# Half of the context tokens' second expert rows: gathered for two tokens at once and added by TensorE in place of VectorE

## The chip, the cores and the metric

The kernel runs on one core of a Trainium2 chip, in one launch. The metric is the time of one execution on the device, in microseconds (us). The engines named here are TensorE (PE in the profile, its weight loads PEld), VectorE (DVE), ScalarE (ACT), GpSimd (POOL) and SyncE (SP); the last two also hold queues from which transfers (DMA) are started.

## The reference

The kernel is one inference step of a two-layer trunk over 128 context tokens and 512 latent tokens of width 1024. In each layer a token mixer (a gated linear attention, a short convolution and a windowed attention, merged by three branch products) is followed by a layer of experts, PEER. What the change touches is that layer, for the context tokens:

```python
def peer_ffn(h, w_pq, keys, u_tab, v_tab):
    ...                                   # 8 heads, top 16 of 128*128 experts each
    gate = jax.nn.softmax(top_s, axis=-1)
    def block(args):
        xb, ib, gb = args                 # 128 tokens, their 8*16 expert indices and gates
        act = jax.nn.gelu(jnp.einsum('td,thkd->thk', xb, u_tab[ib]), approximate=False)
        return jnp.einsum('thk,thkd->td', gb * act, v_tab[ib])
```

So each token has 128 ranks (8 heads times 16). For every rank a row of 1024 numbers of `u_tab` is multiplied with the token (the first half of an expert), and a row of `v_tab` is added to the output with the weight gate times gelu (the second half).

## The kernel before

The tokens stand on the 128 partitions. For the 128 context tokens of a layer, `peer_gather` fetches rows by an indirect transfer from GpSimd's queue: `fetch` starts one transfer of 128 rows, one for each token (512 KB), into a buffer named `grow`. `u_row` (line 920) reads it with one VectorE instruction that multiplies and sums into a column of `w`; `v_row` (lines 930 and 932) reads it with one VectorE instruction that adds it to the accumulator `gacc`. A layer has 128 fetches of each kind, 256 in all, in a fixed sequence: 16 of u, then 16 of u and 16 of v by turns of a head. The use of a row stands one step (`LAG = 1`) behind its fetch, and five `grow` buffers go round (`n=5`).

This gather of layer l is a background generator. While the latent tokens' mixer of the same layer (`mixer_lat`) is written out, each of its products calls `tick()`, and for each tick so many steps of the gather are written between: `RATE`, which is 0.9, 5.5 and 2.464 steps a tick in layer 0 in the three stages (gated attention; windowed attention; branches and output product), and 0.84, 6.0 and 2.08 in layer 1. A tick of the branch stage is 24 matmuls of 512 columns. After that a scheduler orders each engine's instructions. VectorE's gather instructions are kept in program order (`pin`). The order of every engine is fixed when the program is built, and each engine takes its queue strictly in order: what stands behind an instruction that waits, waits too.

Beside the gather, VectorE, ScalarE and GpSimd split each weight unit into two parts in `w_unit` (lines 172 to 176; GpSimd does 5/16 of the low part in these stages), and TensorE takes three matmuls for each product of the latent tokens (lines 196 to 198). PSUM has four pairs of banks (`pa`, `po`, `pb`, `pt`); `pt` holds transposes. Matmuls of 32 columns at four column places of the array, which the change uses, are in the kernel before too: `modulation` (line 267) does them with float32 operands of 128x32 and 128x256.

Of the kernel before, what the change touches and what calls it, by code (L numbers as in the profile page):

```python
# [9 lines left out]
F32 = mybir.dt.float32  # L10
F32R = mybir.dt.float32r
BF16 = mybir.dt.bfloat16
I32 = mybir.dt.int32
U32 = mybir.dt.uint32
U8 = mybir.dt.uint8
AF = mybir.ActivationFunctionType
# [27 lines left out]
def kernel(ctx: ExitStack, tc: tile.TileContext, A: dict, O: list):  # L44
    nc = tc.nc
# [28 lines left out]
    def pt(shape, name="pt"):  # L74
        return psum.tile(shape, F32, tag="pt", name=name, bufs=2)

    act = nc.scalar.activation
    V = nc.vector


    idf = const.tile([128, 128], F32, name="idf")
# [31 lines left out]
    def behind(i, j):  # L113

        tc.add_manual_dep(i.ins, j.ins.name, mybir.DependencyInfo(mybir.DependencyClass.NoSync,
                                                                  mybir.DependencyReason.DATA))
# [662 lines left out]
    def top16(v, ix, x):  # L779
        V.max(v[:, 0:8], x)  # L780
        V.max_index(ix[:, 0:8], v[:, 0:8], x)
        V.match_replace(x, v[:, 0:8], x, NEG)
        V.max(v[:, 8:16], x)
        V.max_index(ix[:, 8:16], v[:, 8:16], x)

    def routing_keys(s, l, hH, hL, vals, idxs, qp):

        for u in range(8):
# [8 lines left out]
            for t in range(s.nt):  # L797
# [7 lines left out]
                    top16(vals[t][:, hp, :], idxs[t][:, hp, :], sc[:, f, :])  # L805
                yield

    def routing_pairs(t, vals, idxs, rp, qp, out):

        vf = vals[t].rearrange("p (h q) k -> p h q k", q=2)
        xf = qp.tile([128, 8, 2, 16], F32, name="xf", bufs=1)
        V.tensor_copy(xf.rearrange("p h q k -> p (h q k)"), idxs[t].rearrange("p h k -> p (h k)"))
        top = qp.tile([128, 8, 16], F32, name="top", bufs=1)
        pos = qp.tile([128, 8, 16], U32, name="pos", bufs=1)
        for h in range(0, 8, 2):
            hs = slice(h, h + 2)
            cand = qp.tile([128, 2, 256], F32, tag="oh", name="cand", bufs=1)[:, :, :136]
            V.tensor_add(cand[:, :, :128].rearrange("p h (a b) -> p h a b", b=16),  # L820
                         vf[:, hs, 0, :8, None].to_broadcast([128, 2, 8, 16]),
                         vf[:, hs, 1, None, :].to_broadcast([128, 2, 8, 16]))
            V.tensor_add(cand[:, :, 128:], vf[:, hs, 0, 8:], vf[:, hs, 1, 0:1].to_broadcast([128, 2, 8]))
            for i in range(2):
                top16(top[:, h + i, :], pos[:, h + i, :], cand[:, i, :])
            yield
        pf = qp.tile([128, 8, 16], F32, name="pf", bufs=1)
        V.tensor_copy(pf, pos)
        ab = qp.tile([128, 2, 8, 16], U32, name="ab", bufs=1)
        V.tensor_scalar(ab[:, 0], pos, 4, None, op0=OP.logical_shift_right)  # L830
        V.tensor_scalar(ab[:, 1], pos, 15, None, op0=OP.bitwise_and)
        abf = qp.tile([128, 2, 8, 16], F32, name="abf", bufs=1)
        V.tensor_copy(abf, ab)

        V.tensor_scalar(pf, pf, -128.0, 0.0, op0=OP.add, op1=OP.max)
        V.tensor_add(abf[:, 0], abf[:, 0], pf)
        V.tensor_sub(abf[:, 1], abf[:, 1], pf)
        sel = rp.tile([128, 2, 8, 16], F32, name="sel%d" % t)
        yield
        for q in range(2):  # L840
            for h in range(0, 8, 2):
                hs = slice(h, h + 2)
                oh = qp.tile([128, 2, 16, 16], F32, tag="oh", name="oh", bufs=1)
                V.tensor_tensor(oh, abf[:, q, hs, :, None].to_broadcast([128, 2, 16, 16]),
                                iota16[:, None, None, :].to_broadcast([128, 2, 16, 16]), op=OP.is_equal)
                V.tensor_mul(oh, oh, xf[:, hs, q, None, :].to_broadcast([128, 2, 16, 16]))
                V.reduce_sum(sel[:, q, hs, :], oh, axis=mybir.AxisListType.X)
                if h % 4 == 2:
                    yield
        flat3 = lambda v: v.rearrange("p h k -> p (h k)")  # L850
        eidx = None
        if t == 0:
            eidx = rp.tile([128, 8, 16], I32, name="eidx")
            V.scalar_tensor_tensor(eidx, sel[:, 0], 128.0, sel[:, 1], op0=OP.mult, op1=OP.add)
            eidx = flat3(eidx)
        gate = rp.tile([128, 8, 16], F32, name="gate%d" % t)
        V.tensor_sub(gate, top, top[:, :, 0:1].to_broadcast([128, 8, 16]))
        act(gate, gate, AF.Exp)
        gs = qp.tile([128, 8], F32, name="gs", bufs=1)
        V.reduce_sum(gs, gate, axis=mybir.AxisListType.X)  # L860
        V.reciprocal(gs, gs)
        V.tensor_mul(gate, gate, gs[:, :, None].to_broadcast([128, 8, 16]))
        out[t] = (eidx, flat3(gate), flat3(sel[:, 0]), flat3(sel[:, 1]))
        yield
# [18 lines left out]
    gcfg = {}  # L883

    def peer_gather(s, l, t, eidx, gate, gp, out=None, after=None):
        h = gp.tile([128, D], F32, name="gh", bufs=1)
        def row():
            return gcfg["p"].tile([128, D], F32, tag=gcfg["tag"], name="grow", bufs=gcfg["n"])

        def mrow(j):  # L890
            t_ = row()
            m = modrow[l][s.idx, j * D:(j + 1) * D]
            nc.sync.dma_start(t_, bass.AP(tensor=m.tensor, offset=m.offset, ap=[[0, 128], [1, D]]))
            return t_

        sc, sh = mrow(4), mrow(3)
        x = s.x[t]
        if not s.ctx:
            x = row()
            nc.sync.dma_start(x, xdr[s.name][:, t, :])  # L900
        i = V.scalar_tensor_tensor(h, sc, 1.0, x, op0=OP.add, op1=OP.mult)
        if after:
            behind(i, after)
        V.tensor_add(h, h, sh)
        acc = gp.tile([128, D], F32, name="gacc", bufs=1)
        junk = gp.tile([128, D], BF16, name="gjunk", bufs=1)
        w = gp.tile([128, 128], F32, name="gw", bufs=1)

        def pin(i):
            if PIN[gcfg["m"]]:  # L910
                tc.keep_in_program_order(i)

        def fetch(tab, j):
            g = row()
            nc.gpsimd.indirect_dma_start(out=g, out_offset=None, in_=A[tab + str(l)],  # L915
                                         in_offset=bass.IndirectOffsetOnAxis(ap=eidx[:, j:j + 1], axis=0))
            return g

        def u_row(j, g):
            pin(V.scalar_tensor_tensor(junk, g, 1.0, h, op0=OP.mult, op1=OP.mult, accum_out=w[:, j:j + 1]))  # L920
            if j % 16 == 15:
                ws = w[:, j - 15:j + 1]
                act(ws, ws, AF.Gelu)

        def v_row(j, g):
            if j % 16 == 0:
                ws = w[:, j:j + 16]
                V.tensor_mul(ws, ws, gate[:, j:j + 16])
            if j == 0:
                pin(V.tensor_scalar(acc, g, w[:, j:j + 1], None, op0=OP.mult))  # L930
            else:
                pin(V.scalar_tensor_tensor(acc, g, w[:, j:j + 1], acc, op0=OP.mult, op1=OP.add))  # L932


        rows = []
        for hd in range(9):
            r = range(hd * 16, hd * 16 + 16)
            rows += [(u_row, "peer_u", j) for j in r if hd < 8] + [(v_row, "peer_v", j - 16) for j in r if hd]
        todo = []
        for i in range(len(rows) + LAG):  # L940
            if i < len(rows):
                todo.append(fetch(*rows[i][1:]))
            if i >= LAG:
                use, _, j = rows[i - LAG]
                use(j, todo.pop(0))
            yield
        if s.ctx:
            peer_add(s, t, [acc], mrow(5), acc)
            normalize(s, [t])
        else:  # L950
            out.append(acc)
# [199 lines left out]
    def run(gen):  # L1151
        for _ in gen:
            pass
# [101 lines left out]
    LAG = 1  # L1255
# [75 lines left out]

    for l in range(DEPTH):
        with pool("g_ctx") as gp:
            gcfg.update(p=gp, tag="grow", n=5, m=0)
            with w_pool(2, 2, PL[1]):
                if l:
                    lat.open_cv()
                    run(lat.finish(l))
                    e = bg_add(peer_gather(C, l, 0, ro_c[0], ro_c[1], gp, after=lat.end), RATE[l][0], PR[2])
                    mixer_lat(l, e, range(4))  # L1340
                else:
                    first = First(gp)
                    e = bg_add(first.work(), RATE[0][0], PR[2])
                    mixer_lat(l, e, range(CONV[0], 4), first)
            bg_drain(e)
# [4 lines left out]
        with pool("e_lat") as ep:  # L1350
            hH, hL = lat.h
            vals, idxs = route_bufs(Lt, ep)
# [156 lines left out]
```

## Time and profile before

| | |
|---|---|
| median of 3 runs | 5698.48 us (5694.15 to 5700.12) |
| the profiled execution | 5700.02 us, its span 5698.2 us |
| TensorE busy | 5144.1 us (90%) |
| VectorE busy | 4257.4 us (75%) |
| GpSimd busy | 2493.1 us (44%) |
| ScalarE busy | 2052.4 us (36%) |
| mean granted TensorE clock | 0.951 of full speed |

The span is what the profiler saw from the first to the last instruction; the execution's own time is 1.8 us longer. Busy shares are means over stages with different limits, so the argument goes by stretches of the span. The context gather of layer 0 runs from 574 us to about 1425 us, that of layer 1 from 3243 us to about 4198 us.

### The profile page before, as it was taken

The page shows a single profiled execution, that of the slowest core. Times are in us where ns is not written, and L with a number is a line of the kernel's source. Part 1 is how long each engine was busy: PE and PEld are TensorE (multiplying, and loading weights), DVE is VectorE, ACT ScalarE, POOL GpSimd, SP SyncE. Part 2 cuts the span into 40 slices and gives each one's busy share as a digit, 9 for nine tenths or more (in the row PEclk, how much of TensorE's full clock was granted, in tenths as well). Part 3 has the DMA queues.
Part 4 walks back from the last instruction along what each step waited for, and adds up shares of the span by engine and source line. Part 5 has one row for each costly group of instructions (what it writes and reads, how often), then busy time and mean ns, then how long its engine had stood idle before and what let it go on. Part 6 is the DMA issues. An engine that isn't in the chain of part 4 may idle for free. (4 is left out here: it accounts for less than half of the span.)

```text
span 5698.2 us, 78492 instructions
## 1 busy us (share of the span) xinstructions
PE 5144.1 (90%) x28598; PEld 4475.9 (79%) x28598; DVE 4257.4 (75%) x7555; ACT 2052.4 (36%) x3456; POOL 2493.1 (44%) x1907
## 2 busy tenths in 40 slices
PE   8998899888899998899999788999989788899997
PEld 6887778767788998888777677777778788799876
DVE  3328878878554868887777798888879998677667
ACT  2214434221232226653333344332223457333332
POOL 1112434676210007876555533456750466444332
PEclk9999999999899999999999899999989899999999
DMA  7762457887666667899999533678842776888895
GB/s 293 269 240 94 156 176 231 297 293 259 212 213 237 226 229 269 307 338 323 325 309 325 186 132 123 225 258 294 293 158 101 233 266 246 310 273 271 285 320 198
DMA packets 456708, 1395.09 MB, mean 245 GB/s; under 512 B 42880, under 2 KB 184832, under 8 KB 413312
## 3 DMA queue, kind: packets, MB, share of 16 engines
q1 hardware_dynamic: 303248, 833.73, 41.3%
q0 software_dynamic: 153072, 556.34, 28.7%
q8 instruction: 225, 3.69, 0.3%
q14 instruction: 163, 1.34, 0.1%
HBM read 1275.29 MB, written 114.62 MB: 244 GB/s over the span
## 5 line engine op out<-in xcount | busy, mean ns | idle before, releaser
L915 POOL DMA_INDIRECT grow<-in_peer_u_dram,eidx x512 | 689.1, 1346 | 675.8 <-DVE gjunk L920 235.8
L915 POOL DMA_INDIRECT grow<-in_peer_v_dram,eidx x512 | 669.3, 1307 | 630.2 <-DVE gacc L932 282.5
L932 DVE SCALAR_TENSOR_TENSOR gacc<-grow,gw,gacc 128x1024 f32<-128x1024 f32 x508 | 707.1, 1392 | 94.8 <-DMA grow<-in_peer_v_dram,eidx 89.8
L176 POOL TENSOR_TENSOR wl<-wraw,wh 128x640 fp32r<-128x640 f32 (+1 forms) x260 | 417.0, 1606 | 703.0 <-ACT wh L172 646.9
L920 DVE SCALAR_TENSOR_TENSOR gjunk<-grow,gh 128x1024 bf16<-128x1024 f32 x512 | 678.1, 1324 | 60.8 <-DMA grow<-in_peer_u_dram,eidx 56.6
L172 ACT ACTIVATE wh<-wraw 128x1024 fp32r<-128x1024 f32 (+1 forms) x388 | 515.2, 1342 | 522.8 <-PE pa L197 207.4
L174 DVE TENSOR_TENSOR wl<-wraw,wh 128x1408 fp32r<-128x1408 f32 (+2 forms) x388 | 555.5, 1434 | 177.2 <-ACT wh L172 177.0
L196 PE MATMUL acc<-wh,daH 128*128 128x512 f32 x1536 | 610.9, 398 | 60.3 <-ACT daH L110 43.8
L198 PE MATMUL acc<-wh,daL 128*128 128x512 f32 x1536 | 612.7, 399 | 14.6 <-DVE daL L111 14.3
L197 PE MATMUL acc<-wl,daH 128*128 128x512 f32 x1536 | 608.4, 396 | 0.5 <-DVE wl L174 0.5
L196 PE MATMUL pa<-hH,wh 128*128 128x512 f32 x1312 | 544.0, 415 | 48.0 <-DVE th L742 12.3
L198 PE MATMUL pa<-hH,wl 128*128 128x512 f32 x1312 | 536.5, 410 | 7.2 <-DVE wl L174 7.2
L197 PE MATMUL pa<-hL,wh 128*128 128x512 f32 x1312 | 536.8, 409 | 0.5 <-DVE hL L111 0.4
L196 PE MATMUL po<-hH,uH 128*128 128x384 f32 x1376 | 490.5, 356 | 26.6 <-ACT uH L1012 10.6
L198 PE MATMUL po<-hH,uL 128*128 128x384 f32 x1376 | 476.6, 347 | 18.4 <-DVE uL L1014 18.1
L197 PE MATMUL po<-hL,uH 128*128 128x384 f32 x1376 | 474.5, 345 | 0.0
L1012 ACT ACTIVATE uH<-uraw 128x1024 fp32r<-128x1024 f32 x256 | 270.8, 1058 | 563.3 <-PE po L197 192.7
L196 PEld LDWEIGHTS acc<-wh,daH 128*128 128x128 f32 x1536 | 294.2, 192 | 130.6 <-ACT daH L110 55.3
L1014 DVE TENSOR_TENSOR uL<-uraw,uH 128x1024 fp32r<-128x1024 f32 (+1 forms) x256 | 285.4, 1115 | 120.0 <-ACT uH L1012 120.0
L985 POOL TENSOR_SCALAR ob<-iota,tt,tt 128x128 f32<-128x128 f32 x192 | 299.3, 1564 | 172.6 <-ACT tt L966 91.8
L198 PEld LDWEIGHTS acc<-wh,daL 128*128 128x128 f32 x1536 | 294.2, 192 | 94.3 <-DVE daL L111 33.4
L196 PEld LDWEIGHTS pa<-hH,wh 128*128 128x128 f32 x1312 | 255.3, 195 | 115.6 <-DVE th L742 14.3
(365 smaller groups left out, 11788.5 us busy)
## 6 DMA issues: line engine op xcount, KB each, us to landing
wraw<-in_w_in_dram SPq DMA_DIRECT2D x168, 1024.0 KB, 5.7
uraw<-in_u_T_dram SPq DMA_DIRECT2D x256, 512.0 KB, 4.7
wraw<-in_v_n_dram SPq DMA_DIRECT2D x256, 512.0 KB, 6.1
wraw<-in_w_mod_dram SPq DMA_DIRECT2D x48, 1024.0 KB, 6.0
wraw<-in_w_branch_dram SPq DMA_DIRECT2D x48, 1024.0 KB, 5.6
gdr<-stage SPq DMA_DIRECT2D x24, 2048.0 KB, 10.4
G<-gdr SPq DMA_DIRECT2D x64, 768.0 KB, 8.0
sdr<-ust SPq DMA_DIRECT2D x172, 192.0 KB, 4.4
```

The lines of the kernel that those rows point to most:

```text
L172: act(H, raw, AF.Copy)
L174: V.tensor_sub(L[:, :m], raw[:, :m], H[:, :m].bitcast(F32))
L176: nc.gpsimd.tensor_sub(L[:, m:], raw[:, m:], H[:, m:].bitcast(F32))
L196: nc.tensor.matmul(out, aH, bH, start=start, stop=False)
L197: nc.tensor.matmul(out, aH, bL, start=False, stop=False)
L198: nc.tensor.matmul(out, aL, bH, start=False, stop=stop)
L915: nc.gpsimd.indirect_dma_start(out=g, out_offset=None, in_=A[tab + str(l)], in_offset=bass.IndirectOffsetOnAxis(ap=eidx[:, j:j + 1], axis=0))
L920: pin(V.scalar_tensor_tensor(junk, g, 1.0, h, op0=OP.mult, op1=OP.mult, accum_out=w[:, j:j + 1]))
L932: pin(V.scalar_tensor_tensor(acc, g, w[:, j:j + 1], acc, op0=OP.mult, op1=OP.add))
L985: (nc.gpsimd if w == "P" else V).tensor_scalar(ob[:, k, :], iota128, TT[1][:, j:j + 1], TT[2][:, j:j + 1], op0=OP.is_equal, op1=OP.mult)
L1012: act(uH, raw, AF.Copy)
L1014: V.tensor_sub(uL[:, :m, :], raw[:, :m, :], uH[:, :m, :].bitcast(F32))
```

## The change

For the context tokens, the second halves of ranks 0 to 63 are fetched in another shape. One fetch brings the 64 rows of token 2f on partitions 0 to 63 and those of token 2f+1 on partitions 64 to 127 (64 such fetches of 512 KB instead of 64 fetches of one rank for 128 tokens; the indices come from `pairs_below`, a TensorE transpose and two VectorE copies). `pair_row` adds them up with TensorE: four float32 matmuls of 128x32 by 128x256, one for each quarter of the width, each at its own column place, whose stationary operand `gdiag` holds the weights of the two tokens in two columns. Sixteen such fetches fill 32 tokens in one PSUM tile `pg` of the `pt` pair; then ScalarE copies it out and four transfers of SyncE's queue put it into `gacc`. The sequence of a layer's 256 fetches is now: 64 of u; 64 times one of u and one pair; 64 of v for ranks 64 to 127, which VectorE adds as before. The use stands two steps behind its fetch instead of one, and there are four `grow` buffers instead of five. The latent tokens' gather keeps its sequence.

```diff
+    def pairs_below(dst, src, copy):
+        p = pt([128, 128], name="pp")
+        nc.tensor.transpose(p, src, idf)
+        for i in range(2):
+            hs = slice(64 * i, 64 * i + 64)
+            copy(dst[hs, :], p[hs, i::2])
...
+            if len(vals) == 1:
+                ef = qp.tile([128, 2, 64], F32, name="pf", bufs=1)
+                V.tensor_copy(ef, eidx[:, None, :64].to_broadcast([128, 2, 64]))
+                e2 = rp.tile([128, 64], I32, name="eidx2")
+                pairs_below(e2, ef.rearrange("p i k -> p (i k)"), V.tensor_copy)
+                eidx = eidx, e2
...
+        def pair_row(f, g):
+            b, i = divmod(f, 16)
+            if f == 0:
+                w2 = gp.tile([128, 2, 64], F32, name="gw2", bufs=1)
+                V.tensor_mul(w2, w[:, None, :64].to_broadcast([128, 2, 64]),
+                             gate[:, None, :64].to_broadcast([128, 2, 64]))
+                wT = gp.tile([128, 64], F32, name="gwT", bufs=1)
+                pairs_below(wT, w2.rearrange("p i k -> p (i k)"), V.tensor_copy)
+                diag = gp.tile([128, 16 * 32], F32, name="gdiag", bufs=1)
+                nc.gpsimd.memset(diag, 0.0)
+                pr.update(w=wT, diag=diag)
+            diag = pr["diag"]
+            if i == 0:
+                for h in range(2):
+                    hs = slice(64 * h, 64 * h + 64)
+                    act(diag[hs, h::34], pr["w"][hs, 16 * b:16 * b + 16], AF.Copy)
+                pr["p"] = pt([128, 256], name="pg")
+            for c in range(4):
+                nc.tensor.matmul(pr["p"][32 * c:32 * c + 32, :], diag[:, 32 * i:32 * i + 32],
+                                 g[:, 256 * c:256 * c + 256], start=i == 0, stop=i == 15,
+                                 tile_position=(0, 32 * c), skip_group_check=True)
+            if i == 15:
+                st = gp.tile([128, 256], F32, name="gst", bufs=1)
+                act(st, pr["p"], AF.Copy)
+                for c in range(4):
+                    nc.sync.dma_start(acc[32 * b:32 * b + 32, 256 * c:256 * c + 256], st[32 * c:32 * c + 32, :])
...
-        for hd in range(9):
-            r = range(hd * 16, hd * 16 + 16)
-            rows += [(u_row, "peer_u", j) for j in r if hd < 8] + [(v_row, "peer_v", j - 16) for j in r if hd]
+        lag = LAG
+        if s.ctx:
+            lag = 2
+            eidx, e2 = eidx
+            rows = [(u_row, "peer_u", eidx, j) for j in range(64)]
+            for j in range(64):
+                rows += [(u_row, "peer_u", eidx, j + 64), (pair_row, "peer_v", e2, j)]
+            rows += [(v_row, "peer_v", eidx, j) for j in range(64, 128)]
...
-            gcfg.update(p=gp, tag="grow", n=5, m=0)
+            gcfg.update(p=gp, tag="grow", n=4, m=0)
```


The scheduler's order shows what this does on two engines.

GpSimd's queue, in the branch stage of layer 0, before. `DMASW0` to `DMASW7` are eight counters that successive fetches use in turn; the counter in a fetch's wait is that of the fetch that filled its buffer the last time, `DVE` or `PE` is the engine that read it then. `wl` is GpSimd's part of a weight unit.

```order
L915 DMA grow<-in_peer_u_dram,eidx 128x1024 [waits DMASW5_49,DVE_49]
L915 DMA grow<-in_peer_u_dram,eidx 128x1024 [waits DMASW6_49,DVE_49]
L915 DMA grow<-in_peer_u_dram,eidx 128x1024 [waits DMASW7_49,DVE_49]
L915 DMA grow<-in_peer_u_dram,eidx 128x1024 [waits DMASW0_49,DVE_49]
L176 TENSOR_TENSOR wl<-wraw,wh 128x640 [waits DMAHW2_49,PE_49,Activation_49]
L915 DMA grow<-in_peer_u_dram,eidx 128x1024 [waits DMASW1_49,DVE_49]
L915 DMA grow<-in_peer_u_dram,eidx 128x1024 [waits DMASW2_49,DVE_49]
```

And in the changed program (`eidx_4315` is `eidx2`, the indices of the pairs):

```order
L930 DMA grow<-in_peer_u_dram,eidx 128x1024 [waits DMASW7_49,DVE_49]
L176 TENSOR_TENSOR wl<-wraw,wh 128x640 [waits DMAHW7_49,Activation_49]
L930 DMA grow<-in_peer_v_dram,eidx_4315 128x1024 [waits DMASW4_49,PE_49]
L930 DMA grow<-in_peer_u_dram,eidx 128x1024 [waits DMASW1_49,DVE_49]
L930 DMA grow<-in_peer_v_dram,eidx_4315 128x1024 [waits DMASW6_49,PE_49]
L930 DMA grow<-in_peer_u_dram,eidx 128x1024 [waits DMASW3_49,DVE_49]
L930 DMA grow<-in_peer_v_dram,eidx_4315 128x1024 [waits DMASW0_49,PE_49]
L176 TENSOR_TENSOR wl<-wraw,wh 128x640 [waits DMAHW3_49,Activation_49]
L930 DMA grow<-in_peer_u_dram,eidx 128x1024 [waits DMASW5_49,DVE_49]
L930 DMA grow<-in_peer_v_dram,eidx_4315 128x1024 [waits DMASW2_49,PE_49]
```

Before, each fetch waits for the fetch five places back, whose row VectorE read. Now a fetch of u waits for the fetch two places back, which is the fetch of u before it: the waits of the u fetches go up by two (7, 1, 3, 5), as their own counters do. The u rows pass through one buffer here, and the pairs go round in the other three, each waiting for TensorE.

TensorE's queue, in the windowed attention of layer 0, in the changed program (`pa` is a product of the convolution; before, the same rows stand without the fifth):

```order
L198 MATMUL pa<-hH,wl 128x512
L196 MATMUL pa<-hH,wh 128x512
L197 MATMUL pa<-hL,wh 128x512
L198 MATMUL pa<-hH,wl 128x512
L970 MATMUL pg<-grow,gdiag 32x256 x12
L196 MATMUL pa<-hH,wh 128x512
L197 MATMUL pa<-hL,wh 128x512
```

Four matmuls are one pair row, so three pair rows stand here in a row. In the branch stage one pair row stands behind every 24 matmuls of 512 columns, and two behind every fourth or fifth such group. Over both layers the 128 pair rows stand in 109 places.

## Rows read from the trace of the kernel before

**Rows 1.** the page: the span, and busy time, share and instructions of each engine

```profile
span 5698.2 us, 78492 instructions
PE 5144.1 (90%) x28598; PEld 4475.9 (79%) x28598; DVE 4257.4 (75%) x7555; ACT 2052.4 (36%) x3456; POOL 2493.1 (44%) x1907
```

**Rows 2.** busy time of each engine in four stretches (start:end, length, engines), clock, DMA

```profile
core 0: us, PE busy (x) PEld busy (x) DVE busy (x) ACT busy (x) POOL busy (x), PEclk, DMA share, GB/s
888.00:1036.00 148.00, 144.67 (x850) 117.75 (x849) 129.32 (x208) 61.79 (x121) 69.18 (x59) 1.00 0.71 229
1036.00:1229.00 193.00, 172.10 (x719) 136.90 (x718) 158.54 (x169) 46.59 (x45) 144.45 (x98) 0.94 0.88 320
3631.00:3874.00 243.00, 223.04 (x1255) 181.89 (x1254) 211.28 (x340) 92.22 (x179) 127.62 (x109) 0.96 0.75 251
3874.00:3967.00 93.00, 82.75 (x339) 65.94 (x339) 75.58 (x80) 21.75 (x21) 64.33 (x43) 0.93 0.90 329
```

**Rows 3.** the same view for gathered rows alone: stretch, VectorE, GpSimd (xcount), clock, DMA

```profile
888.00:1036.00 148.00, 60.04 (x66) 57.69 (x48) 1.00 0.71 229
1036.00:1229.00 193.00, 113.60 (x125) 110.15 (x80) 0.94 0.88 320
3631.00:3874.00 243.00, 115.15 (x135) 109.16 (x91) 0.96 0.75 251
3874.00:3967.00 93.00, 54.06 (x59) 50.62 (x36) 0.93 0.90 329
```

**Rows 4.** VectorE groups, 888 to 1229 us: instruction, count, busy us, mean ns, idle before

```profile
L932 DVE SCALAR_TENSOR_TENSOR gacc<-grow,gw,gacc 128x1024 f32<-128x1024 f32 x64 | 88.9, 1389 | 16.0 <-DMA grow<-in_peer_v_dram,eidx 15.5
L920 DVE SCALAR_TENSOR_TENSOR gjunk<-grow,gh 128x1024 bf16<-128x1024 f32 x64 | 85.5, 1335 | 7.8 <-DMA grow<-in_peer_u_dram,eidx 6.8
```

**Rows 5.** gathers, issue to landing, stretches 888, 1036, 3631 and 3874

```profile
DMA to landing us min/median/max: 4.2/5.4/7.7
DMA to landing us min/median/max: 4.6/6.4/9.8
DMA to landing us min/median/max: 4.1/5.7/9.0
DMA to landing us min/median/max: 5.0/8.0/11.9
```

**Rows 6.** VectorE in order of time around 1140 us: start, duration, instruction

```profile
1137.99 2.59 DVE L920 SCALAR_TENSOR_TENSOR gjunk<-grow,gh 128x1024 bf16<-128x1024 f32 x1
1140.51 0.08 DVE L920 DVE_READ_ACCUMULATOR gjunk<-grow,gh 128x1 f32 x1
```

**Rows 7.** GpSimd in order of time, same place; in brackets the idle time before

```profile
1131.79 0.96 POOL L915 DMA_INDIRECT grow<-in_peer_u_dram,eidx  x1 [0.30 <-issue]
1133.05 0.96 POOL L915 DMA_INDIRECT grow<-in_peer_u_dram,eidx  x1 [0.30 <-issue]
...
1140.86 1.81 POOL L915 DMA_INDIRECT grow<-in_peer_u_dram,eidx  x1 [1.36 <-DVE gjunk L920]
```

**Rows 8.** TensorE in order of time, two places with 32-column matmuls

```profile
1493.46 0.63 PE L267 MATMUL pb<-wraw,cT 128*32 128x256 f32 x6
1494.03 0.66 PE L305 MATMUL pt<-idf,xctx 128*128 128x128 f32 x4
...
1603.73 0.33 PE L197 MATMUL po<-hL,uH 128*128 128x384 f32 x1
1603.90 0.34 PE L198 MATMUL po<-hH,uL 128*128 128x384 f32 x1
1604.17 1.07 PE L267 MATMUL pb<-wraw,cT 128*32 128x256 f32 x16
1605.17 1.13 PE L194 MATMUL pa<-wraw,hF 128*128 128x256 f32 x4
```

**Rows 9.** what TensorE waited for, 888 to 1229 us: us in total, times, longest

```profile
PE pa L196 <- ACT yH L110: 13.0, 3, 7.4
```

**Rows 10.** the page, DMA issues of weights: count, KB each, us to landing

```profile
wraw<-in_w_in_dram SPq DMA_DIRECT2D x168, 1024.0 KB, 5.7
```

More of the change, by code (lines that the diff above doesn't have):

```diff
@@ L911, in pin, with fetch @@
                 tc.keep_in_program_order(i)
-        def fetch(tab, j):
+        def fetch(tab, eidx, j):
             g = row()
@@ new lines, in peer_gather @@
+        pr = {}
+        rows = []
+        lag = LAG
[6 more added lines that the diff above has]
+            rows += [(v_row, "peer_v", eidx, j) for j in range(64, 128)]
+        else:
+            for hd in range(9):
+                r = range(hd * 16, hd * 16 + 16)
+                rows += [(u_row, "peer_u", eidx, j) for j in r if hd < 8]
+                rows += [(v_row, "peer_v", eidx, j - 16) for j in r if hd]
@@ L939, in peer_gather @@
         todo = []
-        for i in range(len(rows) + LAG):
+        for i in range(len(rows) + lag):
             if i < len(rows):
                 todo.append(fetch(*rows[i][1:]))
-            if i >= LAG:
-                use, _, j = rows[i - LAG]
+            if i >= lag:
+                use, _, _, j = rows[i - lag]
                 use(j, todo.pop(0))
```

## The prediction

> **What bounds the kernel now.** The page comes first: the span is 5698.2 us, TensorE is busy for 90% of it and VectorE for 75% [rows 1]. Means over stages say little, so the next view is the table by stretches, cut where the change cuts the gather. The pairs take the places of fetches 66 to 192 of a layer's 256. In layer 0 these run from 888 to 1229 us, in layer 1 from 3631 to 3967 us; I cut each in two where the branch stage takes over: 48 and 80 fetches in layer 0, 91 and 36 in layer 1 [rows 3]. Call the stretches A0 (148 us), B0 (193), A1 (243) and B1 (93): 677 us in all. In them TensorE is busy for 144.67, 172.10, 223.04 and 82.75 us, together 623 us or 92%, VectorE for 575 us or 85% [rows 2]. The list of waits shows that TensorE's idle time is a few waits for ScalarE's or VectorE's part of a split, the largest group 13.0 us in three waits [rows 9]; none is for a gathered row, which TensorE doesn't read. So TensorE sets the pace, with 54 us of slack, and VectorE comes close behind. The gather hangs on VectorE: a fetch that GpSimd held back starts when VectorE has read the row whose buffer it takes [rows 6, 7].
>
> **What is removed.** 128 additions by VectorE, 64 a layer, at 1389 ns [rows 4]: 178 us of VectorE in these stretches. At most TensorE's own idle time can come back from that, 54 us; I take half, since a part of it waits for ScalarE.
>
> **What TensorE gets.** The trace of before has the same matmuls in the modulation. Six records (three float32 matmuls, two records each) start at 1493.46 us and the next matmul at 1494.03: 0.57 us. Sixteen records (eight matmuls, two pair rows) start at 1604.17 and the next at 1605.17: 1.00 us. The matmul ahead of them started 0.27 us earlier, where 0.17 us is its spacing [rows 8]. So a pair row that stands alone costs 0.57 + 0.10 = 0.67 us, and a second one behind it 0.43. By the order the 128 pair rows, some of them split, stand in 109 places and need 151 passes over the four column places: 109 x 0.24 + 151 x 0.43 = 91 us. By stretch that is 17 (A0), 26 (B0), 36 (A1) and 12 (B1).
>
> Those rows show that 32-column work overlaps in the four places and that entering and leaving it costs. The Trainium skill, "TensorEngine Tiling (Array Packing)", section "Tiling Modes", has the rule that speaks against this change: changing the tiling mode drains the engine. The trace agrees, with 0.24 us a place: 26 us of the 91; counting the passes alone the sum would be 65.
>
> With half of the idle time given back, TensorE needs 164 us in A0, 208 in B0, 269 in A1 and 100 in B1, if no row comes late: 64 us more than before.
>
> **What the gather gets.** This is the term on which the forecast rests. Before, five buffers go round, and a fetch has four others between it and the row it replaces. In the changed order of the branch stage the fetches of u pass through one buffer and the pairs through three. A fetch of u can start only when the u before it has landed and VectorE has read it; GpSimd's queue is in order, so the pair behind it waits as well, and TensorE waits for the pair. The cost of one such link: the landing, 6.4 us in the middle in the branch stage [rows 5]; VectorE's reading, 1.34 us [rows 4]; and 0.28 us from VectorE's end (1137.99 + 2.59) to GpSimd's start at 1140.86 [rows 6, 7]. That is 8.0 us, in A0 and A1 with landings of 5.4 and 5.7 us 7.0 and 7.3 us. Where a fetch follows a free buffer it costs GpSimd's pitch, 1.26 us [rows 7]. I followed each stretch's fetches back from the last, each to the reader of its buffer or to the fetch ahead of it, whichever ends later:
> - A0: 15 links and 15 pitches, 15 x 7.0 + 15 x 1.26 = 124 us. TensorE's 164 is longer: +16 us.
> - B0: 32 and 10, 32 x 8.0 + 10 x 1.26 = 269 us against TensorE's 208: +76 us over the 193 before.
> - A1: 28 and 26, 28 x 7.3 + 26 x 1.26 = 237 us against 269: +26 us.
> - B1: 15 and 4, 125 us against 100: +32 us. (The landings of 8.0 us in the middle there, under a DMA share of 0.90, I don't take: a slower stretch moves fewer bytes in a microsecond. They would make it 149.)
>
> The sum is +150 us. In A0 and A1 neither side is slack all the way: three pair rows stand together in TensorE's queue and hold three of four buffers, so that the next three come after a u link and a landing, 7.0 + 5.4 us at least, while TensorE has mostly 8 to 18 us of other work between. Nothing in the trace prices that; between 0 and 60 us (some 15 such places in layer 1, up to 4 us short) I take 20, an estimate.
>
> A rule speaks for a shorter link. The Trainium skill, "DMA: Bandwidth & Descriptors", section "Anatomy of one DMA", fits a transfer from GpSimd's queue as 2.0 us plus its bytes at 436 GB/s, which is 3.2 us for 512 KB, an estimate from that page. By it B0's chain would be 32 x 4.8 + 13 = 166 us and TensorE alone would count. The rows differ: the shortest landing of the four stretches is 4.1 us, the middle ones 5.4 to 8.0.
>
> **What costs nothing, and its cover.** Index and weight preparation is two transposes, some ten small VectorE copies and one clearing by GpSimd a layer; the copies of `pg` and of the weights are 12 ScalarE instructions a layer, and ScalarE is busy for 222 of the 677 us [rows 2]. Without that cover they would be about 10 us. The eight groups of transfers into `gacc` stand in SyncE's queue ahead of weight loads and wait there for TensorE's sixteenth row. I take 0, as loads run ahead; without that cover a load of 5.7 us comes late eight times, 46 us [rows 10]. The tile `pg` leaves one bank of the `pt` pair for the attention's transposes: from 0 up, inside the upper end. Ahead of the pairs and behind them, where all rows go to VectorE, four buffers still go round, and 65 fetches through them (16 links) are far shorter than the time that they have: 0.
>
> **The sum.** 150 + 20 = 170 us on the profiled execution's own 5700 us (1.5 us above the median of the runs): 5870 us.
>
> **The rivals.**
> - TensorE's new work alone counts, and the gather keeps up: +64 us, 5764 us. For it speaks the rule on transfers above, and that landings are shorter where less is moved (5.4 us at a DMA share of 0.71). It decides at landings under 4.5 us, where 32 links and 13 us fit into B0's 208. Against it: 4.6 is the shortest in B0 before.
> - Worse: the bursts cost their 60 us, and SyncE's queue its 46: 5700 + 150 + 106 = 5956 us.
> - Faster: VectorE paces these stretches, and TensorE's busy time is partly stretched by it. If half of the 178 us came back, and the gather kept up, it would be 5611 us. For it speaks VectorE's 85%. It decides where TensorE's true need in the stretches is under 677 - 91 = 586 us, which is 37 us less than it is shown busy; against it is that it is hardly ever seen to wait there.
> - No change: relief and new work cancel, with a gather that keeps up; that needs all 54 us of idle time and 37 more.
>
> **How the numbers follow.** The gather paces the branch stages (5790 to 5930 us): 0.60. TensorE's work alone (5720 to 5790): 0.17. Worse (5930 to 6060): 0.14. Faster: 0.05. Within 0.2%, which is 11 us and about what a measurement of this kernel can tell from no change: 0.04. So slower by more has 0.91. The point is the likeliest case's, 5870. The range 5755 to 5985 holds that case, the upper half of the second (0.10) and most of the worse one (0.11).
>
> **What would show it.** In the changed profile the waits of TensorE in the stretches of pairs should name the transfer into `grow`, with over 100 us in all, most of it in B0 and B1; GpSimd should wait for VectorE's u rows; B0 should be about 269 us and VectorE's busy share there well under 82%. The pair matmuls should occupy about 0.67 us a place. The prediction is wrong if TensorE waits less than 50 us for gathered rows there (then the links are shorter than the rows of before say), or if the stretches are no longer than before.

## The result, and the profile after

The changed kernel takes 5867.79 us (median of 4, 5862.25 to 5886.73) against 5699.3 us: 3.0% slower, ratio 1.0300, 95% interval 1.0274 to 1.0327. The page and the table by stretches, cut at the same fetches (66, 114 and 192 of layer 0; 66, 157 and 192 of layer 1, by their starts in GpSimd's timeline); these rows answer to [rows 1, 2]:

```profile
span 5860.1 us, 80353 instructions
PE 5247.8 (90%) x29626; PEld 4502.0 (77%) x29626; DVE 4073.5 (70%) x7431; ACT 2060.7 (35%) x3485; POOL 2415.4 (41%) x1909
```

```profile
890.00:1052.00 162.00, 154.02 (x986) 116.01 (x985) 98.37 (x186) 59.12 (x119) 63.57 (x58) 0.99 0.63 209
1052.00:1318.00 266.00, 223.90 (x1083) 160.37 (x1080) 94.48 (x120) 49.31 (x50) 123.64 (x99) 0.90 0.70 239
3729.00:4009.00 280.00, 258.51 (x1614) 191.18 (x1613) 163.57 (x300) 93.63 (x184) 114.18 (x110) 0.98 0.67 220
4009.00:4138.00 129.00, 113.48 (x546) 80.71 (x545) 47.47 (x58) 23.90 (x25) 56.90 (x44) 0.93 0.70 247
sum 837.00, PE 749.90 PEld 548.27 DVE 403.89 ACT 225.96 POOL 358.30; mean PE 187.48 PEld 137.07 DVE 100.97 ACT 56.49 POOL 89.57
```

The stretches grew from 677 to 837 us, by 160 where the span grew by 162. (Counted by the starts of the fetches, as in the table under the experiments, they grew by 165 and the fetches around them by 21; the rest of the span became 24 us shorter, and no run shows why.) A0 went from 148 to 162 us, B0 from 193 to 266, A1 from 243 to 280, B1 from 93 to 129. VectorE, relieved, is busy for 36% of B0.

The same table for the pair matmuls alone:

```profile
890.00:1052.00 162.00, 16.58 (x192) 5.62 (x192) 0.99 0.63 209
1052.00:1318.00 266.00, 24.75 (x316) 6.92 (x312) 0.90 0.70 239
3729.00:4009.00 280.00, 35.09 (x360) 11.03 (x360) 0.98 0.67 220
4009.00:4138.00 129.00, 11.74 (x144) 2.98 (x144) 0.93 0.70 247
```

They make 88 us, where the prediction had 17, 26, 36 and 12. B0 grew by 73 us: 25 are pair matmuls, 21 are waits (42 us of idle time for the 21 of before), and 27 are the kernel's own matmuls, since the stretch holds more of them (767 records for 719) and each takes 0.260 us for 0.239. In the four stretches together TensorE's idle time grew from 54 to 87 us. The list for TensorE in B0 (us in total, times, longest), which answers to [rows 9]:

```profile
PE pa L196 <- DVE th L742: 10.8, 3, 4.6
PE pg L970 <- DMA grow<-in_peer_v_dram,eidx: 8.9, 7, 5.3
PE pa L196 <- DVE mg L742: 8.3, 3, 4.0
PE pa L197 <- DVE yL L111: 7.8, 2, 4.8
PE pa L196 <- ACT yH L110: 6.2, 2, 5.9
```

The same list for VectorE there:

```profile
DVE gjunk L935 <- DMA grow<-in_peer_u_dram,eidx: 169.7, 38, 8.3
```

TensorE's five waits make 42.0 us, all that B0 has beside its 223.9 busy. Only 8.9 of it names a gathered row; 26.9 name a piece of VectorE's (`th` and `mg`, the merging of the branches, and `yL`, a split). VectorE itself stood 169.7 us waiting for rows of u. How one becomes the other is seen in the timeline, first VectorE, then GpSimd, then TensorE:

```profile
1150.33 1.23 DVE L935 SCALAR_TENSOR_TENSOR gjunk<-grow,gh 128x1024 bf16<-128x1024 f32 x1 [4.29 <-DMA grow<-in_peer_u_dram,eidx]
1151.48 0.68 DVE L742 SCALAR_TENSOR_TENSOR mg<-th,pa 128x512 f32<-128x512 f32 x1
1157.02 1.22 DVE L935 SCALAR_TENSOR_TENSOR gjunk<-grow,gh 128x1024 bf16<-128x1024 f32 x1 [4.86 <-DMA grow<-in_peer_u_dram,eidx]
```

```profile
1151.83 0.95 POOL L930 DMA_INDIRECT grow<-in_peer_u_dram,eidx  x1 [2.14 <-DVE gjunk L935]
1153.09 0.93 POOL L930 DMA_INDIRECT grow<-in_peer_v_dram,eidx  x1 [0.30 <-issue]
1158.52 0.93 POOL L930 DMA_INDIRECT grow<-in_peer_u_dram,eidx  x1 [4.50 <-DVE gjunk L935]
```

```profile
1149.79 0.64 PE L970 MATMUL pg<-grow,gdiag 128*32 128x256 f32 x8
1152.22 0.50 PE L196 MATMUL pa<-hH,wh 128*128 128x512 f32 x1 [1.78 <-DVE mg L742]
```

The row of u that VectorE wants at 1146 lands at 1150.33. VectorE's queue is in order, so `mg` behind it runs at 1151.48, and TensorE, whose next product goes into PSUM space that `mg` reads, at 1152.22. The next fetch of u starts at 1151.83, when its only buffer is read, and the one after at 1158.52: a link of 6.69 us. Over the 29 places in B0 where a fetch of u waits for the u before it, two fetches back, a link takes 7.16 us in the middle and 7.48 in the mean, by the starts of the two fetches.

### The profile page after: what moved, and what is told of

Same layout as the page of the kernel before. It is cut to its first block, busy times and chain, and to the rows that moved or that the text cites. A ratio compares the mean times of both kernels' runs of the same rounds, so it can differ in the third digit from the quotient of the medians.

```text
span 5860.1 us, 80353 instructions
## 1 busy us (share of the span) xinstructions
PE 5247.8 (90%) x29626; PEld 4502.0 (77%) x29626; DVE 4073.5 (70%) x7431; ACT 2060.7 (35%) x3485; POOL 2415.4 (41%) x1909
## 5 line engine op out<-in xcount | busy, mean ns | idle before, releaser
L930 POOL DMA_INDIRECT grow<-in_peer_u_dram,eidx x512 | 645.0, 1260 | 837.7 <-DVE gjunk L935 459.5
L930 POOL DMA_INDIRECT grow<-in_peer_v_dram,eidx x512 | 651.5, 1272 | 702.6 <-DVE gacc L947 213.0
L935 DVE SCALAR_TENSOR_TENSOR gjunk<-grow,gh 128x1024 bf16<-128x1024 f32 x512 | 665.2, 1299 | 389.7 <-DMA grow<-in_peer_u_dram,eidx 387.4
L176 POOL TENSOR_TENSOR wl<-wraw,wh 128x640 fp32r<-128x640 f32 (+1 forms) x260 | 388.4, 1496 | 713.4 <-ACT wh L172 678.9
L947 DVE SCALAR_TENSOR_TENSOR gacc<-grow,gw,gacc 128x1024 f32<-128x1024 f32 x382 | 538.6, 1410 | 108.3 <-DMA grow<-in_peer_v_dram,eidx 99.2
```

Of the source, the lines that this page charges most:

```text
L176: nc.gpsimd.tensor_sub(L[:, m:], raw[:, m:], H[:, m:].bitcast(F32))
```

## The experiments

The theory (links): u has one buffer, so that each of its fetches waits for a landing and a reading, and VectorE's and TensorE's queues wait behind. The rivals: TensorE's own new work; the number of buffers, four for five; the sequence and the lag.

**Own buffers, the same four.** The edit:

```diff
-            g = row()
+            if s.ctx and eidx is e2:
+                g = gp.tile([128, D], F32, tag="growp", name="growp", bufs=2)
+            else:
+                g = row()
-            gcfg.update(p=gp, tag="grow", n=4, m=0)
+            gcfg.update(p=gp, tag="grow", n=2, m=0)
```

> The changed kernel with the same four buffers, but two kept for u rows and two for pairs. Links theory (a u fetch through one buffer waits for the u before it, and VectorE's and TensorE's queues wait behind): by the order the chain of fetches is 99 us in A0, 169 in B0, 197 in A1 and 75 in B1, all shorter than TensorE's 164, 208, 269 and 100. So B0 falls from 266 us to 205 to 225, B1 from 129 to 98 to 110, A0 and A1 change by less than 20 us: 5770 to 5800 us. Work theory (TensorE's passes and changes of place set the time, 128 pairs in both): no change, 5850 to 5885. Theory of the number of buffers (four are too few): no change either. Waits of VectorE for u rows in B0 go from 170 us to under 60 by the links theory.

5974.15 us, slower than the changed kernel (ratio to before 1.0497, 1.0466 to 1.0528). The total misses, since I had overlooked that the rows of VectorE ahead of the pairs and behind them were left with two buffers as well. The table shows each stretch by the starts of the fetches in GpSimd's timeline (us; the flanks are the 66 and 63 fetches around the pairs of each layer; the cuts of [rows 2] lie up to 5 us off them; the first fetch of layer 1 in the kernel before starts at 3232.9 us, not at 3243):

| | ahead 0 | A0 | B0 | behind 0 | ahead 1 | A1 | B1 | behind 1 |
|---|---|---|---|---|---|---|---|---|
| before | 317 | 149 | 189 | 177 | 401 | 243 | 91 | 186 |
| after | 321 | 162 | 266 | 178 | 408 | 280 | 129 | 195 |
| own buffers | 354 | 157 | 227 | 237 | 429 | 264 | 111 | 269 |
| own, flanks by turns | 319 | 162 | 229 | 186 | 408 | 280 | 110 | 200 |
| one for u | 338 | 181 | 284 | 238 | 432 | 311 | 135 | 253 |
| two u, three pairs | 334 | 167 | 212 | 179 | 396 | 259 | 117 | 191 |

The pair stretches fell by 78 us, as the links theory says (B0 and B1 ended 2 us and 1 us above their ranges, and VectorE's waits for rows of u in B0 fell to 53.5 us, under the 60 expected), and the flanks grew by 187. So the next run lets the flanks use all four.

**The same, flanks by turns** (a fetch there with an odd rank takes `growp`, one with an even rank `grow`).

> The earlier version with two buffers for u and two for pairs, but the rows ahead of the pairs and behind them, all VectorE's, take the two kinds of buffers by turns, so that all four go round there; in the run before they had two, and those parts grew by 187 us while the pair stretches fell by 78. Links theory: the pair stretches stay at 157, 227, 264 and 111 us (within 10), the flanks go back to the changed kernel's 321, 178, 408 and 195 us: 5775 to 5805 us. Theory that TensorE's work alone sets the 168 us: 5850 to 5885.

5835.24 us, 33 less than the changed kernel (ratio 1.0237, 1.0217 to 1.0257), and 30 above the expected range. B0 and B1 keep their gain of 56 us; A0 and A1 lost theirs. Of TensorE's waits in B0 one kind is left:

```profile
PE pg L974 <- DMA growp<-in_peer_v_dram,eidx: 26.6, 9, 5.2
```

VectorE's wait for u rows fell to 56.4 us there. The wait has changed sides: with two buffers the pairs are late. TensorE doesn't wait for VectorE any more, and B0's 230 us are 203.9 of busy TensorE and this.

**One buffer for u, by force** (`n=1` for `grow`, three for `growp`, flanks by turns).

> Four buffers, one kept for u and three for pairs (the flanks by turns), so that every fetch of u among the pairs is a link of the chain, not 28 to 32 of 42 in the branch stages. By the order the chains are 158, 299, 308 and 137 us at the prediction's links, and 158, 269, 304 and 124 at the 7.2 us that the changed kernel showed in B0 (128, 264, 237, 120 for the changed kernel at the prediction's). Links theory: A1 grows from 280 to 305 to 330 us, B0 from 266 to 270 to 300, B1 to 125 to 140: 5895 to 5955 us. Theory that pairs wait and u rows don't matter (three buffers for pairs as now): 5850 to 5880. TensorE's work alone: the same.

6080.67 us (ratio 1.0662, 1.0636 to 1.0688). The pair stretches grew by 74 us to 911; A1, B0 and B1 came out as the links theory expected, A0, for which it named no time, at 181. The total misses by 126, since the flanks by turns send every second row through the one buffer: the flanks grew by 159 us, a slip of the same kind as in the first run. The view of the row buffers in its branch stage shows the theory at its plainest, who waited and for how many times:

```profile
its engine sat idle before it (us, times) until:
  DMA grow<-in_peer_u_dram,eidx: 184.0, 38
  DVE gjunk L939: 139.7, 37
```

All 38 rows of u find VectorE waiting, and 37 of 38 fetches find GpSimd waiting for VectorE.

**Room for a fifth buffer, and the control.** Five don't fit beside the change's tiles, so room is made: `u_row` writes its product over the row instead of into `gjunk`, the weights go into a part of `gw`, and `gw2` shares `gst`'s space.

```diff
-            pin(V.scalar_tensor_tensor(junk, g, 1.0, h, op0=OP.mult, op1=OP.mult, accum_out=w[:, j:j + 1]))
+            pin(V.scalar_tensor_tensor(g if s.ctx else junk, g, 1.0, h, op0=OP.mult, op1=OP.mult, accum_out=w[:, j:j + 1]))
...
-                wT = gp.tile([128, 64], F32, name="gwT", bufs=1)
+                wT = w[:, :64]
```

> A control for the next run: the changed kernel with four buffers, u_row's product written into the row's own buffer instead of a bf16 tile, and three small tiles folded into others (2.75 KB a partition come free). Every theory expects the changed kernel's time, 5855 to 5885 us; by the order its chains are 131, 264, 243 and 120 us against 128, 264, 237 and 120.

5891.04 us (1.0349, 1.0318 to 1.0379): 23 us above the changed kernel, 6 over the range. Of the 28 us between the two profiled spans only 7 lie in the context gather; where the others come from isn't shown. What the five-buffer runs give is read against this one.

> The control with a fifth buffer in the common ring. By the order u still passes through one buffer in 22 of B0's 39 fetches of u (29 before), and the chains are 108, 239, 226 and 116 us. Links theory: B0 falls by 20 to 30 us and B1 by 4 to 8, little else: 5825 to 5850 us. Theory of the number of buffers: with before's five the wait goes, B0 near 208 and B1 near 100: 5770 to 5800. Work theory: no change, 5850 to 5885.

5856.74 us (1.0283, 1.0253 to 1.0313), 34 less than the control. The theory of the number of buffers wanted 5770 to 5800, so that a fifth buffer in a common ring helps little. The total lies 7 us above the range of the links theory and inside that of the work theory, but both had been set from the changed kernel. Read against the control the change is clear of noise, and the work theory expected none; by the starts of the fetches B0 fell from 271 to 259 us and B1 from 125 to 118, where the links theory wanted 20 to 30 and 4 to 8. That it is so little because u still passes through one buffer in 22 of B0's 39 fetches is an argument here; the next run, with the same five buffers divided, tests it.

**Five buffers, two for u and three for pairs.**

> With the room made as in the control (5891 us, 23 above the changed kernel), five buffers: two for u, three for pairs, the flanks by turns. With two and two, TensorE still waited 50 us for pairs in the pair stretches (26.6 of them in B0). If the second pair buffer is what that hangs on, 30 to 50 us go: 5835 + 23 - 40 = 5818, 5800 to 5835 us. If it hangs on how late a pair is started behind VectorE's u rows, nothing goes: 5850 to 5870.

5786.94 us (1.0144, 1.0127 to 1.0161): 104 us less than the control with four, 70 less than the same five buffers in a common ring, and 13 under the range of the case in which the second pair buffer decides. B0's row of the table by stretches, and what TensorE waited for there:

```profile
1068.00:1280.00 212.00, 200.11 (x1047) 143.48 (x1045) 108.76 (x121) 48.56 (x49) 132.95 (x100) 0.98 0.84 297
```

```profile
PE pg L974 <- DMA growp<-in_peer_v_dram,eidx: 9.7, 3, 7.2
PE pa L197 <- DVE yL L111: 1.3, 1, 1.3
PE pa L196 <- DVE mg L742: 1.0, 1, 1.0
```

TensorE is busy for 94% of B0. It is the fastest version that adds up all the pairs, and still slower than before.

**VectorE's old additions in the new sequence** (in the list of rows `pair_row` is replaced by `v_row` of the same rank; lag two, four buffers).

> The changed kernel's sequence (64 of u; u and v by turns; 64 of v), its lag of two and its four buffers, but the second halves of ranks 0 to 63 are fetched one rank at a time for 128 tokens and added by VectorE as before; TensorE gets no pairs. Links theory: all rows are released by VectorE in turn, so the four buffers go round (fetch n waits for n-4), the chain is 153 us in B0 against TensorE's 182, and the time is that of before, 5690 to 5720 us. Theory of the sequence or of the four buffers: most of the 168 us stays, 5800 to 5870. Work theory: as before, 5690 to 5720, since the pairs are gone.

5747.38 us (1.0087, 1.0055 to 1.0119), 51 above before: neither 5690 to 5720, nor most of the 168. So something in the frame of the change costs TensorE time without pairs. The next run takes it apart.

**Before with four buffers** (`n=5` becomes `n=4`).

> The kernel before with four buffers in place of five, nothing else. The run with the new sequence and VectorE's old additions came out 51 us above before, where 0 to 20 were expected. If the fifth buffer is what it lost, this one does too: 5735 to 5755 us, with VectorE waiting for rows in the two branch stages some 75 to 115 us (65 with five). If the sequence and the lag cost it: 5690 to 5712 us.

5766.15 us (1.0117, 1.0094 to 1.0139), 66 above before and 11 over the expected range: the fifth buffer is the cost, and beside it the sequence and the lag cost nothing that shows (the two intervals overlap). VectorE's waits for rows in the two branch stages, 65 us with five buffers, are 133 us, layer 0 first:

```profile
DVE gjunk L920 <- DMA grow<-in_peer_u_dram,eidx: 39.6, 17, 4.3
DVE gacc L932 <- DMA grow<-in_peer_v_dram,eidx: 38.9, 18, 4.9
...
DVE gacc L932 <- DMA grow<-in_peer_v_dram,eidx: 35.9, 19, 7.7
DVE gjunk L920 <- DMA grow<-in_peer_u_dram,eidx: 18.2, 12, 3.8
```

**TensorE's work without the fetches.** All pair matmuls read the tile of the tokens (`gh`), and no pair is fetched:

```diff
+            if s.ctx and eidx is e2:
+                return h
             g = row()
```

> The changed kernel without the pairs' fetches: all pair matmuls read the tile of the tokens' normalized values, which is there anyway (the pairs' sums are left out of the output). u has all four buffers, nothing waits for a pair. This is TensorE's new work and VectorE's relief alone. Links theory: the prediction's rival price, 5700 + 91 - 27 = 5764 us, 5740 to 5780. Work theory: the changed kernel's 5868, 5840 to 5885.

5745.82 us (1.0074, 1.0051 to 1.0097), in the range of the links theory and 94 us below that of the work theory. With no pair to fetch, TensorE's work still makes this 51 us slower than before. The page:

```profile
span 5744.3 us, 80093 instructions
PE 5215.8 (91%) x29626; PEld 4489.6 (78%) x29626; DVE 4089.7 (71%) x7431; ACT 2063.9 (36%) x3487; POOL 2327.3 (41%) x1781
```

Against the changed kernel's page, for the same number of matmuls, the span is 116 us shorter: 84 us of that are idle time of TensorE, and 32 are busy time (the mean granted clock is 0.954 for 0.950). In the pair stretches VectorE's waits for rows fall from 346 us to 0.9, and TensorE's waits that name VectorE from 47 us to 4.3. So nearly all of TensorE's waiting for VectorE there goes when no row of u is late.

**The relief alone** (the pairs' additions are left out too).

> The same without the pair matmuls as well: of ranks 0 to 63 the second halves are left out altogether, one clearing of the accumulator in their place. VectorE's relief alone, and 128 transfers less. By the prediction's term at most TensorE's idle 54 us come back, half of them taken: 5673 us, 5655 to 5700. The rival that VectorE paces these stretches: 5700 - 89 = 5611 us. The difference from the run with matmuls is the price of TensorE's work: 91 us by the sum of places and passes (70 to 100).

5649.67 us (0.9918, 0.9895 to 0.9942). This is 5 us under the expected range. So the relief, with 128 transfers less and four buffers for the rows that are left, is worth 45 us by its own runs of before (5695 us), not 89. The work is worth 96 us by the two medians, 89 by the two ratios (0.0156 of 5699).

**The passes cut to an eighth**, without and with fetches (`:32` in place of `:256` in the matmul's columns, and the copy repeats them). First without fetches; the run that took 29 us is the one told after it.

> The run without pair fetches (5746 us; 96 us above the one without matmuls), its pair matmuls cut to 32 of 256 columns (seven eighths of those products left out). In the run with own buffers the same cut took 29 us where 40 to 60 were expected. If passes cost 0.43 us each as the prediction has it, 57 us go here, where nothing waits for a row: 5680 to 5700 us, and the 29 were short because waits took their place. If a pass costs half as much, 5710 to 5725 us, and the changes of place cost more than 0.24 us each.

5689.45 us (0.9978, 0.9969 to 0.9988): 56 us less than with full columns, where 57 were expected. Over 151 passes that is 0.43 us a pass, if its time goes with its columns.

Now with fetches, in the run with own buffers and flanks by turns.

> The same, but a pair's four matmuls read 32 of their 256 columns each (so that seven eighths of the pairs' sums are left out; the rest of the copied tile repeats the first columns). All fetches, waits and changes of place stay. With the links gone TensorE should pace: 151 passes of 0.43 us shortened by seven eighths give 57 us, so 40 to 60 us under the run with full columns, 5725 to 5760 us. If something else paces there (VectorE's reading of u, the landing of pairs), less than 15 us.

5805.96 us (1.0179, 1.015 to 1.0208): 29 less, under the expected 40 to 60 and over the 15 of the other case. TensorE's waits for pairs in the four stretches are 6.0, 19.7, 25.6 and 8.8 us, 60 in all against 50 with full columns, so 10 us of the shorter work went into waiting for pairs. The granted clock in A0 and A1 is 0.94 and 0.94 against 0.99 and 0.96. That the two explain the whole difference is an argument, not shown.

## Why the prediction was right

The steps in the order of the prediction:

- **TensorE's work, 91 us: right.** The pair matmuls are busy for 88 us in the stretches; the runs without fetches give 96 or 89; cutting the passes gave 56 us for 57. A place, by the timeline of the run without fetches, here a pair row alone:

```profile
1109.82 0.40 PE L198 MATMUL pa<-hH,wl 128*128 128x512 f32 x1
1110.14 0.64 PE L972 MATMUL pg<-gh,gdiag 128*32 128x256 f32 x8
1110.71 0.50 PE L196 MATMUL pa<-yH,wh 128*128 128x512 f32 x1
```

  The matmul behind starts 0.89 us after the one ahead, where 0.23 us is the spacing: 0.66 us for 0.67. The Trainium skill, "TensorEngine Tiling (Array Packing)", section "Tiling Modes", says that a change of tiling mode drains the engine; the trace agrees in that the change costs time, with 0.09 us more than spacing ahead of the pair (0.32 less 0.23) and 0.57 us from its start to the next.
- **What comes back from VectorE, 27 us: undersized.** 45 us came back, with 128 transfers less in the same run, which no run here tells apart. It is far from the 89 of the rival in which VectorE paces.
- **The gather paces the branch stages: right in place and nearly in size, half wrong in the way.** The step was 106 us above TensorE's work (170 less 64); 5867.79 less 5745.82 is 122. By stretch the forecast was +16, +76, +26 and +32, with 20 more for the bursts in A0 and A1; the trace shows +14, +73, +37 and +36. What was wrong is "TensorE waits for the pair": its waits for pairs are 2.0, 8.9, 5.8 and 2.7 us, 19 in all, under the 50 that the prediction itself set as the mark of being wrong. The links are there, of 7.5 us in the mean instead of 8.0, but TensorE pays for them mostly through VectorE: of its 87 us of idle time there, 47 name VectorE (29 before, with VectorE's additions still in its queue). VectorE stands 346 us for rows of u (32.9, 169.7, 65.1 and 78.3), and `th`, `mg`, `yL` are behind it in its queue. The order showed it, and I had named what waits behind the fetch on GpSimd and not what waits behind the reading on VectorE. In B0 and B1 the four runs with own buffers move the stretches as the links say, in both directions.
- **Landings: taken too long.** They are 5.4, 5.5, 5.4 and 5.7 us in the middle for the 5.4, 6.4, 5.7 and 8.0 of [rows 5], at DMA shares of 0.63 to 0.70 where before it was 0.71 to 0.90. That B0's 269 us came out at 266 is in part luck: by the starts of the fetches 29 links make 217 us and the ten other steps, of 2.5 to 9.1 us, make 49, where the prediction had 256 for 32 links and 13 for the pitches. The shortest landing in the changed kernel is 4.0 us; the Trainium skill's "DMA: Bandwidth & Descriptors", section "Anatomy of one DMA", gives 3.2 us for this size, an estimate from that page, and no run here shows it.
- **Four buffers around the pairs, 0: nearly right there.** The flanks grew by 21 us (4, 1, 7 and 9). But the fifth buffer is worth 66 us to the kernel before, and the prediction had no term for it: in the pair stretches it is inside the links, and a change that kept VectorE's additions would have paid it just so.
- **SyncE's queue, 0: right.** Loads of weights land in 5.2 us in the middle in B0, where before it was 7.2, and no wait of TensorE in B0 is for one.

So the 168 us are, by the runs: 45 back, 96 of TensorE's work, and 122 of fetching the pairs through buffers shared with u. (They make 173; the runs of before in the two sets lie 5 us apart, 5695 and 5699.) That 170 came out at 168 is in part luck: the relief was taken 18 us too small and the gather's part 16 us, and the two cancel. Own buffers and a fifth one give back 104 read against the control, 81 of the 122 read against the changed kernel itself. The 41 us between that version and the run without the pairs' fetches no run divides up.

## What to carry to other kernels

When two engines empty a common ring of buffers, look who gets which: here five in common gave 34 us and the same five divided 104. A late row shows under the name of whatever stands behind its reader in an in-order queue, so read the waits of the reader, not only of the engine that paces. Before giving work to the engine that paces, price it with its inputs resident: that run alone (5746 us) says that a gather that is never late would not have made up for these matmuls, as they stand and with four buffers.

## What was not expected of the hardware

TensorE's matmuls can be slower behind a wait, with the engine at work all the time. After the 1.78 us that ended at 1152.22, its matmuls of 512 columns are 0.43 us apart from 1153.26 to 1156.25, and 0.23 us from 1156.66 on. The table by stretches for these two pieces:

```profile
1153.20:1156.20 3.00, 3.00 (x8) 2.31 (x8) 0.00 (x0) 0.00 (x0) 0.82 (x1) 0.50 0.97 345
1156.60:1159.20 2.60, 2.60 (x12) 2.07 (x11) 1.83 (x3) 0.00 (x0) 0.68 (x1) 1.00 0.19 77
```

The granted clock is 0.50, the lower of its levels (1.2 of 2.4 GHz), and then 1.00. The wait of 1.70 us for a pair that ended at 1141.96 is followed in the same way by matmuls 0.43 us apart from 1143.19 to 1145.75. It is not so behind every wait: one of 2.55 us for `mg` ended at 1120.80, and the clock stayed at 1.00 for the 22 us behind it:

```profile
1120.80:1142.90 22.10, 20.01 (x106) 14.26 (x107) 5.84 (x8) 3.00 (x3) 9.58 (x9) 1.00 0.68 248
```

B0 has eight pieces at the lower clock: six begin inside a wait of TensorE of 3.0 to 5.9 us, two about 1 us behind the waits named here. Over B0 the clock is 0.90 in the changed kernel, 0.94 before and 0.98 with two buffers for u and three for pairs; in the run where no pair is fetched it is 1.00 in both layers' stretches:

```profile
887.40:1220.40 333.00, 328.14 (x1929) 243.89 (x1929) 202.54 (x302) 104.49 (x166) 141.25 (x91) 1.00 0.54 187
3660.00:3995.40 335.40, 328.81 (x2022) 246.85 (x2020) 211.31 (x354) 117.25 (x208) 125.59 (x88) 1.00 0.51 173
```

Without the pairs' matmuls B0 counts 767 records in 199.2 busy us in the changed kernel, and 735 in 175.4 with two buffers for u and three for pairs. At the second's rate the first would take 183 us, so by this estimate some 16 us of B0's growth are the slower clock, beside 21 us more of waits.
